# Attention scores as three fp32r passes on 64 rows, and projections pinned between the units of an attention

## The chip, the cores and the metric

One core of a Trainium2 chip. TensorE (PE, with its weight loads shown as PEld), VectorE (DVE), ScalarE (ACT) and GpSimd (POOL) each take their instructions in order and wait for each other through semaphores; SyncE (SP) issues the transfers. The metric is the time of one launch on the device in microseconds; lower is better.

## The reference

A chain of two blocks on 256 tokens of width 1024, all in fp32. The first block (convolution, retention, gated feed-forward, gate) is not touched. The second has two layers on the tokens ("lat") and, in the first layer, on 256 context tokens ("ctx"):

```python
# layer 0: differential attention, 8 heads, each with two score maps of 64 channels
q_l, k_l = apply_rope(q_l, cos, sin), apply_rope(k_l, cos, sin)   # lat only
s = einsum('bqhmd,bkhmd->bhmqk', q_blk, k) * 64 ** -0.5           # m = 0, 1
p = softmax(s);  p = p[:, :, 0] - lam * p[:, :, 1];  o = p @ v    # v: 128 channels
o = rmsnorm(o, subln) * (1 - lam_init);  y = o.reshape(...) @ wo
# lat queries read ctx and lat keys (512), ctx queries read ctx keys (256)
# layer 1: neighbourhood attention, 16 heads of 64 channels, lat queries only
s = concat([q @ k_lat * 64 ** -0.5 + bias (masked), q @ k_ctx * 64 ** -0.5])   # 512 keys
o = softmax(s) @ v;  y = o.reshape(...) @ wo
# after each: h = h + g * y, then a gated feed-forward on rmsnorm(h)
```

## The kernel before

Activations lie with channels on the 128 partitions and tokens in the columns. A projection is a sum of three fp32r products (`mm3`, or `mm3_tok` with tokens and weights exchanged): weights and activations are each split into a rounded part `hi` and the rest `lo`, and hi x hi, hi x lo and lo x hi are summed in PSUM. `weights` loads a tile of 1,024 or 768 columns into one of four buffers `raw`, and makes `hi` on ScalarE (L129) and `lo` on VectorE (L130), five buffers each. One such tile of 1,024 is 24 matmuls of 256 columns.

A scheduler puts each engine's instructions in order when the kernel is built. It goes by the order in the program and fills what is not ready yet with later work; `tc.issue_after(ins)` keeps instructions behind one of the same engine. The order is then fixed: on the chip an engine that waits holds all that is behind it.

**Layer 0.** `early_qk` and `early_v` project the context of head pairs c = 0 to 2 before the tokens are ready. For c = 0 to 3 the main loop then projects the tokens' q and k (128 channels are one head's two maps, j is the head of the pair), rotates them in fp32 (`rope`: L731 to L734, four VectorE steps), projects v, and calls `da_heads`. The projections of pair c + 1 follow the units of pair c in the program, so they are what TensorE has for its waits. `da_unit` works on one head and one block of 128 queries, 32 in all: two score products (L757), one for each map, each in plain fp32 from 64 of the partitions (q and k rows 0 to 63 or 64 to 127), each into one of two PSUM banks `s`; for each map a maximum (L761) and its scaling (L762) on VectorE and an exponential with its sum (L764) on ScalarE; a few one-column steps (L767 to L769); the combination of the two maps (L770); transposes on TensorE (L773), a copy (L775), the product with v (L780); and the RMS norm of the result (L783 to L787, with GpSimd's power at L785), which a later unit's `flush` transposes into `po_all`. The outputs of pairs 0 to 2 are kept as `raws` and split after the last projection, because the split tiles use the ring of the projections' inputs. `wo_first(0)` is the first part of the output projection, eight pieces of 18 matmuls, after all units. `ada_dve(0, 3, ...)` is 16 products on VectorE (L256) for a modulation vector of the next norm.

**Layer 1.** For each c (four heads), q is scaled and cut into `hi` and `lo` halves for each head, laid on opposite halves of the partitions, and k gets three tiles in the same way, by 12 ScalarE and 8 VectorE instructions on half tiles. `na_scores` then needs two matmuls a head and query block (32 in all): one over 128 rows (L989), which sums hi x hi and lo x hi, and one over 64 rows (L990) for hi x lo. Bias (L992), maximum, exponential and scaling follow, then transposes and the product with v. Each head's bias table is fetched into one of three buffers when its head comes.

## Time and profile before

| | |
|---|---|
| median of 3 runs | 1448.93 us (1446.19 to 1449.93) |
| the profiled execution | 1450.36 us, span 1448.1 us |
| busy in the span | PE 1410.9, PEld 1262.8, DVE 1075.4, ACT 700.5, POOL 34.1 us |
| mean granted TensorE clock | 0.991 |
| score products of layer 0 (L757) | 455.3 to 637.9 us, 128 matmuls |
| score products of layer 1 (L989, L990) | 1064.6 to 1229.8 us, 64 matmuls |

The span is from the first to the last instruction of the profiled execution. A matmul's busy time covers its way through the pipeline, so that matmuls overlap; the distance between starts is the rate. A plain fp32 matmul shows as two.

### The profile page before, as it was taken

The numbers are of one execution on the slowest core, as the hardware profiler recorded it, in microseconds if no ns is written. First come the engines' busy times: TensorE is split into PE (matmuls) and PEld (weight loads), VectorE is DVE, ScalarE is ACT, GpSimd is POOL, SyncE is SP. The second block draws the span as 40 slices with busy tenths as digits, with TensorE's granted clock in tenths as the row PEclk, the third lists the DMA queues.
The fourth block names the chain that finished last, engine by engine and source line by source line (L and its number), as shares of the span: only waits on it lengthen the run. The fifth ranks groups of instructions, "written<-read, shape, count | busy, mean of one in ns | idle before, by whom it ended". The sixth has DMA issues, their size and how long they took to land.

```text
span 1448.1 us, 25617 instructions
## 1 busy us (share of the span) xinstructions
PE 1410.9 (97%) x9811; PEld 1262.8 (87%) x9811; DVE 1075.4 (74%) x2333; ACT 700.5 (48%) x1323; POOL 34.1 (2%) x52
## 2 busy tenths in 40 slices
PE   7998999999999999999999999999999999999997
PEld 6898899999998887589888888889988778899997
DVE  7975889985778785778699999965775576676653
ACT  5655544454554545754432222323565555654442
POOL 0000000000000010110000000000000000000000
PEclk9999899999999999999999999999999999999998
DMA  8457498677554331034466676634632233355562
GB/s 289 128 168 255 169 318 275 218 215 221 167 175 146 131 96 32 7 103 160 132 215 198 210 239 218 210 123 129 203 99 87 74 88 119 132 182 182 153 180 91
DMA packets 76874, 236.66 MB, mean 163 GB/s; under 512 B 8656, under 2 KB 13008, under 8 KB 76624
## 3 DMA queue, kind: packets, MB, share of 16 engines
q1 hardware_dynamic: 76752, 235.03, 50.6%
q8 instruction: 77, 1.26, 0.3%
q14 instruction: 45, 0.37, 0.1%
HBM read 233.95 MB, written 1.05 MB: 162 GB/s over the span
## 4 chain that ended last, share of the span: by engine, by line
PE 80%; issue 13%; DMA 2%; DVE 2%; ACT 1%; SPq 0%; POOL 0%; DVEq 0%; POOLq 0%; ACTq 0%
PE mm L161 19%; PE mm L162 19%; PE mm L163 19%; PE s L757 3%; PE mm L172 2%; PE mm L171 2%; PE mm L170 2%; PE t L780 2%; PE o L1022 1%; DMA raw<-w_in 1%; PE s L162 1%; PE s L161 1%; PE s L163 1%; PE t L1012 1%; PE s L990 1%
## 5 line engine op out<-in xcount | busy, mean ns | idle before, releaser
L129 ACT CAST hi<-raw 128x1024 fp32r<-128x1024 f32 (+2 forms) x376 | 358.8, 956 | 547.8 <-PE mm L162 345.7
L130 DVE TENSOR_TENSOR lo<-raw,hi 128x1024 fp32r<-128x1024 f32 (+2 forms) x376 | 415.5, 1106 | 158.1 <-ACT hi L129 154.6
L161 PE MATMUL mm<-x,hi 128*128 128x256 f32 (+2 forms) x1568 | 486.3, 314 | 13.0 <-ACT x L151 7.9
L162 PE MATMUL mm<-x,hi 128*128 128x256 f32 (+2 forms) x1568 | 487.4, 312 | 1.3 <-DVE x L612 1.0
L163 PE MATMUL mm<-x,lo 128*128 128x256 f32 (+2 forms) x1568 | 487.5, 312 | 0.8 <-DVE lo L130 0.8
L161 PEld LDWEIGHTS mm<-x,hi 128*128 128x128 f32 x1568 | 299.9, 193 | 39.7 <-issue 11.4
L163 PEld LDWEIGHTS mm<-x,lo 128*128 128x128 f32 x1568 | 301.9, 193 | 23.5 <-issue 8.6
L162 PEld LDWEIGHTS mm<-x,hi 128*128 128x128 f32 x1568 | 301.9, 193 | 22.2 <-issue 6.1
L256 DVE SCALAR_TENSOR_TENSOR junk<-adaw,sb 128x512 f32<-128x512 f32 x320 | 220.2, 688 | 12.9 <-DMA adaw<-ada 8.5
L161 PE MATMUL mm<-o,hi 128*128 128x256 f32 (+1 forms) x356 | 105.3, 300 | 0.7 <-ACT o L147 0.5
L162 PE MATMUL mm<-o,hi 128*128 128x256 f32 (+1 forms) x356 | 105.6, 298 | 0.0
L163 PE MATMUL mm<-o,lo 128*128 128x256 f32 (+1 forms) x356 | 105.3, 297 | 0.0
L163 PE MATMUL s<-x,lo 128*128 128x258 f32 (+1 forms) x288 | 81.9, 284 | 0.0
L161 PE MATMUL s<-x,hi 128*128 128x258 f32 (+1 forms) x288 | 81.8, 284 | 0.0
L162 PE MATMUL s<-x,hi 128*128 128x258 f32 (+1 forms) x288 | 81.8, 284 | 0.0
L162 PE MATMUL mm<-q,hi 128*128 128x256 f32 (+1 forms) x265 | 81.0, 306 | 0.0
L163 PE MATMUL mm<-q,lo 128*128 128x256 f32 (+1 forms) x265 | 80.9, 305 | 0.0
L161 PE MATMUL mm<-q,hi 128*128 128x256 f32 (+1 forms) x265 | 80.9, 305 | 0.0
L161 PEld LDWEIGHTS mm<-o,hi 128*128 128x128 f32 x356 | 67.4, 191 | 5.4 <-issue 1.7
L162 PEld LDWEIGHTS mm<-o,hi 128*128 128x128 f32 x356 | 68.0, 191 | 2.6 <-issue 0.5
L163 PEld LDWEIGHTS mm<-o,lo 128*128 128x128 f32 x356 | 68.0, 191 | 1.9 <-issue 0.2
L172 PE MATMUL mm<-hi,x 128*128 128x256 f32 x240 | 69.1, 288 | 0.0
(250 smaller groups left out, 2153.9 us busy)
## 6 DMA issues: line engine op xcount, KB each, us to landing
raw<-gu SPq DMA_DIRECT2D x88, 512.0 KB, 3.9
adaw<-ada SPq DMA_DIRECT2D x80, 512.0 KB, 4.5
raw<-wqkv SPq DMA_DIRECT2D x66, 512.0 KB, 4.3
raw<-ffn SPq DMA_DIRECT2D x44, 512.0 KB, 5.6
raw<-down SPq DMA_DIRECT2D x37, 384.0 KB, 3.2
raw<-down SPq DMA_DIRECT2D x37, 320.0 KB, 3.0
raw<-w_in SPq DMA_DIRECT2D x22, 512.0 KB, 5.3
o<-ada SPq DMA_DIRECT2D x32, 256.0 KB, 5.9
```

Source lines behind the costliest of these rows:

```text
L129: last_conv[:] = [act.copy(hi[:, :n], raw[:, :n]).ins, dve.tensor_tensor(lo[:, :n], raw[:, :n], f32(hi[:, :n]), op=ALU.subtract).ins]
L130: dve.tensor_tensor(lo[:, :n], raw[:, :n], f32(hi[:, :n]), op=ALU.subtract).ins]
L161: pe.matmul(out, wh, xh, start=first and k == 0, stop=False)
L162: pe.matmul(out, wh, xl, start=False, stop=False)
L163: last_mm[0] = pe.matmul(out, wl, xh, start=False, stop=last and k == n - 1).ins
L170: pe.matmul(out, xh[:, ts_], wh, start=k == 0, stop=False)
L171: pe.matmul(out, xh[:, ts_], wl, start=False, stop=False)
L172: pe.matmul(out, xl[:, ts_], wh, start=False, stop=k == n - 1)
L256: dve.scalar_tensor_tensor(out=junk, in0=raw[:, gs_], scalar=1.0, in1=sb[:, v, gs_], op0=ALU.mult, op1=ALU.mult, accum_out=acc[:, n, v, g: ...
L757: pe.matmul(o, q[ms, qs], k[ms, k0:k0 + n], start=True, stop=True)
L780: mm = pe.matmul(po[:, :P], pT[:, j * P:(j + 1) * P], vv, start=j == 0, stop=j == nk - 1)
L990: pe.matmul(ps, q[rows, qs], k[2][rows], start=False, stop=True)
```

## The change

Both attentions now split q and k into `hi` and `lo` tiles and make each score map of three fp32r matmuls on 64 rows, hi x hi, hi x lo and lo x hi. The two maps (or two heads) that share a tile are alternated, so that consecutive matmuls use opposite halves of the rows and different banks. `both_free` orders the first matmul of a unit behind the `reciprocal` of the one before it, which follows both exponentials. The scale 1/8 moves into the split of q, and the maximum is negated by the reduction, so that L762 and L994 go; two one-column steps of the norm move to GpSimd.

In layer 0 the projections are cut into pieces of 24 matmuls (one weight tile) and handed to `da_heads` as `fill`: each is traced after one unit, and its matmuls are kept behind that unit's last score matmul. The context's projections of pair 3 become such pieces too, the q and k of a pair are made one head at a time, and `wo_first(0)` becomes eight pieces behind the units of pair 3. The splits of `raws` move: three after the first head of pair 1, one straight from PSUM, two after pair 2. In layer 1 both bias tables of a pair of heads are fetched ahead of its scores.

```diff
-EARLYN = 9
+WO_AT = {1: (0,), 2: (1, 2), 3: (3,), 4: (4,), 5: (5,), 6: (6,), 7: (7,)}
...
+    last_exp = [None]
+    def both_free(mm):
+        if last_exp[0] is not None:
+            tc.add_manual_dep(mm.ins, last_exp[0].name, mybir.DependencyInfo(
+                mybir.DependencyClass.NoSync, mybir.DependencyReason.DATA), reason="both banks")
...
-        p, ps = [], []
-        for m in range(2):
-            ms = slice(64 * m, 64 * m + 64)
-            o = bank(pss, "s")[:, :n]
-            pe.matmul(o, q[ms, qs], k[ms, k0:k0 + n], start=True, stop=True)
-            ps.append(o)
+        (qh, ql), (kh, kl) = q, k
+        ps = [bank(pss, "s")[:, :n] for _ in range(2)]
+        for i, (a_, b_) in enumerate(((qh, kh), (qh, kl), (ql, kh))):
+            for m in range(2):
+                ms = slice(64 * m, 64 * m + 64)
+                mm = pe.matmul(ps[m], a_[ms, qs], b_[ms, k0:k0 + n], start=i == 0, stop=i == 2)
+                if i + m == 0:
+                    both_free(mm)
+        last_s = mm.ins
+        p = []
         for m in range(2):
             o = ps[m]
-            dve.tensor_reduce(out=sc[:, m:m + 1], in_=o, axis=AX.X, op=ALU.max)
-            dve.tensor_scalar(out=sc[:, 2 + m:3 + m], in0=sc[:, m:m + 1], scalar1=-0.125, scalar2=None, op0=ALU.mult)
+            dve.tensor_reduce(out=sc[:, 2 + m:3 + m], in_=o, axis=AX.X, op=ALU.max, negate=True)
             e = tmp2("e", 3)
-            act.activation(e[:, :n], o, AF.Exp, bias=sc[:, 2 + m:3 + m], scale=0.125, accum_out=sc[:, 4 + m:5 + m])
+            act.activation(e[:, :n], o, AF.Exp, bias=sc[:, 2 + m:3 + m], accum_out=sc[:, 4 + m:5 + m])
             p.append(e)
-        dve.reciprocal(sc[:, 7:8], sc[:, 5:6])
+        pool.tensor_tensor(sc[:, 6:7], sc[:, 4:5], sc[:, 4:5], op=ALU.mult)
+        last_exp[0] = dve.reciprocal(sc[:, 7:8], sc[:, 5:6]).ins
         dve.scalar_tensor_tensor(out=sc[:, 8:9], in0=sc[:, 4:5], scalar=sc[:, 7:8], in1=nlam, op0=ALU.mult, op1=ALU.mult)
-        dve.scalar_tensor_tensor(out=sc[:, 6:7], in0=sc[:, 4:5], scalar=sc[:, 4:5], in1=epsc, op0=ALU.mult, op1=ALU.mult)
         dve.scalar_tensor_tensor(out=p[0][:, :n], in0=p[1][:, :n], scalar=sc[:, 8:9], in1=p[0][:, :n], op0=ALU.mult, op1=ALU.add)
...
-        dve.scalar_tensor_tensor(out=sc[:, 10:11], in0=sc[:, 9:10], scalar=1.0 / 128, in1=sc[:, 6:7], op0=ALU.mult, op1=ALU.add)
+        pool.tensor_scalar(out=sc[:, 10:11], in0=sc[:, 6:7], scalar1=128 * EPS, scalar2=sc[:, 9:10], op0=ALU.mult, op1=ALU.add)
...
+        return last_s
...
+    def qk_piece(c, grp, j):
+        def run(ins):
+            part_ = weights(a["wqkv0"][grp * 4 + c][:, j * 1024:(j + 1) * 1024], (1024,))
+            ps = bank(pmm, "mm")
+            with behind(ins):
+                mm3(ps[:, :T], per_k(part_, [KD], P), xl)
+            ring_ = "q" if (c, j) == (3, 1) else "o"
+            raw, hi, lo = tmp2(), slot(ring_, F32R), slot(ring_, F32R)
+            act.copy(raw[:, T:], early[c][grp][:, j * T:(j + 1) * T])
+            rope(raw, ps[:, :T])
+            if grp == 0:
+                split_scaled(raw, 0.125, hi, lo)
+            else:
+                split(raw, hi, lo)
+            QK[c][grp][j] = (hi, lo)
+        return run
...
+            ps, w = open_v[0]
+            with behind(ins):
+                mm3_tok(ps[:, jj * T:(jj + 1) * T], w, xl, CS[jj])
...
+        def fill_in(u, ins):
+            for f in fill.get(u, ()):
+                f(ins)
...
-            raw = slot("o")
-            act.activation(raw, po_all, AF.Copy, scale=sub8)
-            raws.append(raw)
-    for c in range(4):
...
-            if c < 2:
-                ps = bank(pmm, "mm")
-                for j in range(2):
-                    s = got[2 * grp + j]
-                    o = ps[:, j * T:(j + 1) * T]
-                    mm3(o, w[j], xl)
-                    rope(s, o)
-                    dst.append(s)
...
-        if c == 3:
-            for raw in raws:
-                hi, lo = slot("x", F32R), slot("x", F32R)
-                split(raw, hi, lo)
-                os_.append((hi, lo))
-        da_heads(c, q, k, v)
+    for f in (qk_piece(0, 0, 0), qk_piece(0, 1, 0), v_piece(0, 0), v_piece(0, 1)):
+        f(None)
+    for c in range(3):
+        fill = {0: [qk_piece(c, 0, 1)], 1: [qk_piece(c, 1, 1)], 4: [qk_piece(c + 1, 0, 0)], 5: [qk_piece(c + 1, 1, 0)]}
+        if c == 0:
+            fill.update({2: [early_piece(0, 0)], 3: [early_piece(0, 1)], 6: [v_piece(1, 0)], 7: [v_piece(1, 1)]})
+        elif c == 1:
+            fill[0].append(early_piece(1, 0))
+            fill[1].append(early_piece(1, 1))
+            fill.update({2: [early_piece(2, 0)], 3: [early_piece(2, 1)], 6: [v_piece(2, 0)], 7: [v_piece(2, 1)]})
+        else:
+            fill.update({2: [qk_piece(3, 0, 1)], 3: [qk_piece(3, 1, 1)], 6: [v_piece(3, 0)], 7: [v_piece(3, 1)]})
+        da_heads(c, fill)
         if c == ADA3 and 3 not in ADA_PE:
             ada_dve(0, 3, (last_load[0], last_mul[0]), range(ADA3N, KD), *acc3)
+    split_raws()
...
+    def wo_piece(v, n):
+        def run(ins):
+            if n % 2 == 0:
+                open_w[0] = weights(a["wo0a"][n // 2], (768, 768)), bank(pmm, "mm")
+            ws, ps = open_w[0]
+            o = ps[:, (n % 2) * T:(n % 2 + 1) * T]
+            with behind(ins):
+                mm3(o, per_k([ws[n % 2]], (6,), P), part(os_[:6], v))
+            resid(0, 2, n, o, v)
+        return run
     def wo_first(v):
         for n in range(KD):
-            if n % 2 == 0:
-                ws = weights(a["wo0a"][n // 2], (768, 768))
-                ps = bank(pmm, "mm")
-            o = ps[:, (n % 2) * T:(n % 2 + 1) * T]
-            mm3(o, per_k([ws[n % 2]], (6,), P), part(os_[:6], v))
-            resid(0, 2, n, o, v)
-    wo_first(0)
+            wo_piece(v, n)(None)
+    da_heads(3, {u: [wo_piece(0, n) for n in ns] for u, ns in WO_AT.items()})
...
-    def na_scores(q, k, jj, qt, bt):
-        rows = slice(64 * jj, 64 * jj + 64)
-        qs = slice(jj * T + qt * P, jj * T + (qt + 1) * P)
+    def na_scores(q, k, i, qt):
+        (qh, ql), (kh, kl) = q, k
+        qs = slice(i * T + qt * P, i * T + (qt + 1) * P)
+        ps = [bank(pss, "s") for _ in range(2)]
+        for n, (a_, b_) in enumerate(((qh, kh), (qh, kl), (ql, kh))):
+            for jj in range(2):
+                rows = slice(64 * jj, 64 * jj + 64)
+                mm = pe.matmul(ps[jj], a_[rows, qs], b_[rows], start=n == 0, stop=n == 2)
+                if n + jj == 0:
+                    both_free(mm)
+        return ps
+    def na_softmax(ps, qt, bt):
         sc = small.tile([P, 12], F32, tag="sc", name="sc", bufs=8)
-        ps = bank(pss, "s")
-        pe.matmul(ps, q[:, qs], k[jj], start=True, stop=False)
-        pe.matmul(ps, q[rows, qs], k[2][rows], start=False, stop=True)
         b0 = 128 if qt == 0 else 0
         dve.tensor_tensor(ps[:, :T], ps[:, :T], bt[:, b0:b0 + T], op=ALU.add)
-        dve.tensor_reduce(out=sc[:, 0:1], in_=ps, axis=AX.X, op=ALU.max)
-        dve.tensor_scalar(out=sc[:, 1:2], in0=sc[:, 0:1], scalar1=-1.0, scalar2=None, op0=ALU.mult)
+        dve.tensor_reduce(out=sc[:, 1:2], in_=ps, axis=AX.X, op=ALU.max, negate=True)
         e = tmp2("e", 3)
         act.activation(e, ps, AF.Exp, bias=sc[:, 1:2], accum_out=sc[:, 2:3])
-        dve.reciprocal(sc[:, 3:4], sc[:, 2:3])
+        last_exp[0] = dve.reciprocal(sc[:, 3:4], sc[:, 2:3]).ins
         dve.tensor_scalar(out=e, in0=e, scalar1=sc[:, 3:4], scalar2=None, op0=ALU.mult)
...
+            bts = []
             for jj in range(2):
-                bt = tmp2()
-                nc.sync.dma_start(out=bt[:, :384], in_=a["rpb"][4 * c + 2 * i + jj])
-                for qt in range(2):
-                    e = na_scores(q[i], k[i], jj, qt, bt)
+                bts.append(tmp2())
+                nc.sync.dma_start(out=bts[jj][:, :384], in_=a["rpb"][4 * c + 2 * i + jj])
+            for qt in range(2):
+                ps = na_scores(q, k[i], i, qt)
+                for jj in range(2):
+                    e = na_softmax(ps[jj], qt, bts[jj])
...
-            s = slot("q", F32R)
-            for jj in range(2):
-                d = s[:, jj * T:(jj + 1) * T]
-                act.activation(d[H[jj]], o[H[jj]], AF.Copy, scale=0.125)
-                dve.scalar_tensor_tensor(
-                    out=d[H[1 - jj]], in0=o[H[jj]], scalar=0.125, in1=f32(d[H[jj]]), op0=ALU.mult, op1=ALU.subtract)
-            q.append(s)
+            mm3(ps[:, j * T:(j + 1) * T], w[j], xl)
+        q, k = (slot("q", F32R), slot("q", F32R)), []
+        split_scaled(ps, 0.125, *q)
...
-            s = [slot("q", F32R) for _ in range(3)]
-            for jj in range(2):
-                for r in (jj, 1 - jj):
-                    act.copy(s[jj][H[r]], ps[H[jj]])
-                dve.tensor_tensor(s[2][H[jj]], ps[H[jj]], f32(s[jj][H[jj]]), op=ALU.subtract)
+            s = slot("q", F32R), slot("q", F32R)
+            split(ps, *s)
```

## Rows read from the trace of the kernel before

**Rows 1.** Page, chain that ended last: shares of the span by engine.
```profile
PE 80%; issue 13%; DMA 2%; DVE 2%; ACT 1%; SPq 0%; POOL 0%; DVEq 0%; POOLq 0%; ACTq 0%
```

**Rows 2.** Windows (us): length; PE, PEld, DVE, ACT, POOL busy (count); clock; DMA share; GB/s.
```profile
455.00:578.00 123.00, 123.00 (x815) 98.88 (x814) 92.19 (x278) 66.56 (x172) 9.91 (x16) 1.00 0.29 90
578.00:612.00 34.00, 30.85 (x158) 18.57 (x157) 23.49 (x83) 23.91 (x78) 4.32 (x8) 1.00 0.05 15
...
500.00:540.00 40.00, 40.00 (x274) 33.29 (x274) 32.76 (x106) 20.20 (x53) 3.65 (x5) 1.00 0.27 80
1140.00:1180.00 40.00, 40.00 (x253) 32.03 (x252) 22.48 (x48) 20.81 (x45) 0.00 (x0) 1.00 0.26 75
```

**Rows 3.** Timeline, TensorE, differential scores: start, length (us), line, operands, count.
```profile
455.33 1.13 PE L757 MATMUL s<-q 64*128 64x512 f32 x4
...
461.89 0.28 PE L161 MATMUL mm<-x,hi 128*128 128x256 f32 x1
462.01 0.28 PE L162 MATMUL mm<-x,hi 128*128 128x256 f32 x1
462.22 1.12 PE L757 MATMUL s<-q 64*128 64x512 f32 x2
463.27 0.39 PE L163 MATMUL mm<-x,lo 128*128 128x256 f32 x1
463.49 0.28 PE L161 MATMUL mm<-x,hi 128*128 128x256 f32 x1
...
471.74 0.28 PE L171 MATMUL mm<-lo,x 128*128 128x256 f32 x1
471.95 0.70 PE L757 MATMUL s<-q 64*128 64x256 f32 x2
...
472.80 0.28 PE L170 MATMUL mm<-hi,x 128*128 128x256 f32 x1
```

**Rows 4.** Timeline, loads of weights for the product at 462.22.
```profile
462.21 0.29 PEld L757 LDWEIGHTS s<-q 64*128 64x128 f32 x2
```

**Rows 5.** Timeline, TensorE, neighbourhood scores.
```profile
1072.20 0.39 PE L989 MATMUL s<-q 128*128 128x512 f32 x1
1072.52 0.50 PE L990 MATMUL s<-q 64*128 64x512 f32 x1
1072.95 0.39 PE L161 MATMUL mm<-x,hi 128*128 128x256 f32 x1
1073.18 0.28 PE L162 MATMUL mm<-x,hi 128*128 128x256 f32 x1
```

**Rows 6.** Groups by line and shape, 440 to 660: count | busy us, mean ns | idle before.
```profile
L130 DVE TENSOR_TENSOR lo<-raw,hi 128x1024 fp32r<-128x1024 f32 x21 | 25.6, 1220 | 2.0 <-ACT hi L129 1.9
L761 DVE TENSOR_REDUCE sc<-s 128x1 f32<-128x512 f32 x32 | 22.1, 689 | 9.1 <-PE s L757 8.2 <-POOL sc L785 0.8
...
L761 DVE TENSOR_REDUCE sc<-s 128x1 f32<-128x256 f32 x32 | 13.4, 422 | 9.5 <-PE s L757 9.0
L770 DVE SCALAR_TENSOR_TENSOR e<-e,sc 128x512 f32<-128x512 f32 x16 | 12.0, 750 | 0.3
L256 DVE SCALAR_TENSOR_TENSOR junk<-adaw,sb 128x512 f32<-128x512 f32 x16 | 11.0, 685 | 0.0
L762 DVE TENSOR_SCALAR sc<-sc 128x1 f32<-128x1 f32 x64 | 9.4, 148 | 0.3
L770 DVE SCALAR_TENSOR_TENSOR e<-e,sc 128x256 f32<-128x256 f32 x16 | 7.7, 481 | 0.2
...
L769 DVE SCALAR_TENSOR_TENSOR sc<-sc,epsc 128x1 f32<-128x1 f32 x32 | 6.9, 215 | 4.7 <-ACT e L764 4.5
L734 DVE TENSOR_TENSOR q<-rp 128x256 f32<-128x256 f32 x16 | 6.7, 417 | 0.7 <-PE t L780 0.7
...
L148 DVE TENSOR_TENSOR x<-o,x 128x512 fp32r<-128x512 f32 x6 | 4.1, 688 | 1.2 <-ACT x L147 1.0
...
L785 POOL TENSOR_TENSOR sc<-sc,mhalf 128x1 f32<-128x1 f32 x32 | 18.6, 580 | 202.2 <-DVE sc L784 116.5 <-DVE sc L762 85.7
```

More of the change, by code (lines that the diff above doesn't have):

```diff
@@ L639, in body @@
     down("down1", fs, ep)
-    early = [], [], []
+    early = [], [], [], []
     def early_qk(c, grp):
@@ L661, in early_v @@
             mm3_tok(ps[:, j * T:(j + 1) * T], w, xc, CS[j])
-        s = slot("q" if c < 2 else "o")
+        s = slot("q")
         act.copy(s, ps)
         early[c].append(s)
-    steps = [lambda c=c, i=i: early_v(c) if i == 2 else early_qk(c, i) for c in range(3) for i in range(3)][:EARLYN]
+    steps = [lambda c=c, i=i: early_v(c) if i == 2 else early_qk(c, i) for c in range(3) for i in range(3)]
     def early_some(i, j):
@@ L789, in da_unit, with behind @@
         late.append((po_all[:, at:at + P], on))
-    os_, raws = [], []
-    def da_heads(c, q, k, v):
+        return last_s
+    QK = [[[None] * 2 for _ in range(2)] for _ in range(4)]
+    V = [[] for _ in range(4)]
+    def behind(ins):
+        return tc.issue_after(ins) if ins is not None else nullcontext()
+    def qk_piece(c, grp, j):
[14 more added lines that the diff above has]
+        return run
@@ new lines, in body, with v_piece, early_piece, run @@
+    open_v = [None]
+    def v_piece(c, jj):
+        def run(ins):
+            if jj == 0:
+                open_v[0] = bank(pmm, "mm"), w_wide(a["wqkv0"][8 + c])
+            ps, w = open_v[0]
+            with behind(ins):
+                mm3_tok(ps[:, jj * T:(jj + 1) * T], w, xl, CS[jj])
+            if jj == 1:
+                s = slot("q")
+                act.copy(s, ps)
+                V[c] += [s, early[c][2]]
+        return run
+    open_e = [None]
+    def early_piece(i, j):
+        def run(ins):
+            if j == 0:
+                src = a["wqkv0"][i * 4 + 3]
+                open_e[0] = bank(pmm, "mm"), w_wide(src) if i == 2 else w_blocks(src)
+            ps, w = open_e[0]
+            o = ps[:, j * T:(j + 1) * T]
+            with behind(ins):
+                if i == 2:
+                    mm3_tok(o, w, xc, CS[j])
+                else:
+                    mm3(o, w[j], xc)
+            if j == 1:
+                s = slot("q")
+                act.copy(s, ps)
+                early[3].append(s)
+        return run
@@ L794, in da_heads, with split_raws @@
+    os_, raws = [], []
+    def split_raws():
+        for raw in raws:
+            hi, lo = slot("x", F32R), slot("x", F32R)
+            split(raw, hi, lo)
+            os_.append((hi, lo))
+        raws.clear()
+    def da_heads(c, fill):
+        def fill_in(u, ins):
+            for f in fill.get(u, ()):
+                f(ins)
         if c == 3:
-            parts = [(slot("o", F32R), slot("o", F32R)) for _ in range(2)]
+            parts = [(slot("x", F32R), slot("x", F32R)) for _ in range(2)]
+            u = 0
@@ new lines, in da_heads @@
+            if c == 1 and i == 0:
+                raw = slot("q")
+                act.activation(raw, po_all, AF.Copy, scale=sub8)
+                raws.append(raw)
+                split_raws()
+            elif c == 1:
+                hi, lo = slot("x", F32R), slot("x", F32R)
+                split_scaled(po_all, sub8, hi, lo)
+                os_.append((hi, lo))
+            else:
+                raw = slot("q")
+                act.activation(raw, po_all, AF.Copy, scale=sub8)
+                raws.append(raw)
@@ L1025, in na_heads @@
             os_.append((s[:, :T], s[:, T:]))
-    H = slice(0, 64), slice(64, 128)
     for c in range(4):
```

68 lines of the change are left out of this document (17 added, 51 removed).

## The prediction

> **What bounds the kernel now.** I read the chain that ended last first, then the busy times of two stretches, then the TensorE timeline step by step. The chain is TensorE for 80% of the span [rows 1]. Busy time alone says too little, because matmuls overlap in the pipeline; the reader should look at the distance from one matmul's start to the next. In a dense run of 256-column fp32r matmuls that step is 0.12 us, and every score product breaks the rhythm [rows 3]. In differential attention TensorE is dense from 455 to 578 us, with VectorE busy 92.2 of 123 us (75%; the densest slice, 500 to 540 us, has 82%). From 578 to 612 us, where the projections have run out, TensorE has 158 matmuls and 3.2 us with none running [rows 2]. So a score product that gets cheaper shortens the end directly, as long as VectorE and ScalarE deliver the softmax in time.
>
> **Scores of differential attention.** There are 32 units (8 heads, 4 blocks of queries): 16 "lat" units with 512 keys, 16 "ctx" units with 256. Each has two 64-row products in plain fp32, each of which runs as two passes. A 512-key product alone: without it the matmuls at 463.27 and 463.49 would have followed 462.01 by 0.12 and 0.24, as that one follows 461.89; it costs 463.49 - 462.01 - 0.24 = 1.24 us. A 256-key one, with one matmul left out of the rows before 472.80, costs 472.80 - 471.74 - 0.24 = 0.82 [rows 3]. The 0.42 between them is 256 columns in two passes, so an fp32 pass takes 0.21 for 256 columns, and 0.82 - 0.42 = 0.40 is fixed, paid at the change between 128-row and 64-row matmuls. Where both halves of a unit stand side by side, four passes take 1.13 us where two take 1.12 [rows 3]: the two row halves run at the same time. On the timeline 6 such pairs and 52 single products stand (27 of 512 keys, 25 of 256 alone). A pair costs what its longer half costs: 4 hold a 512-key product, 2 do not. Before: 31 x 1.24 + 27 x 0.82 = 60.6 us.
>
> After, a unit is six fp32r passes, alternating between the halves, so three passes' time and one change of mode. An fp32r pass of 256 columns is 0.12. For 512 columns the neighbourhood scores tell it: a 128-row and a 64-row product together cost 1073.18 - 1072.20 - 0.12 = 0.86 [rows 5] (the first, at 1072.20, would itself have been the next step), which is two passes and the fixed 0.40, so 0.23 a pass. A lat unit: 0.40 + 3 x 0.23 = 1.09; a ctx unit: 0.40 + 3 x 0.12 = 0.76. After: 16 x 1.85 = 29.6 us. **Saved: 31.0 us.** Bounds: nothing hides better than this from below; from above, if the fp32r halves did not overlap, six passes make 1.78 and 1.12, 46.4 us, 14.2 saved.
>
> The three passes need their weights loaded behind a running pass in the same half. The row for the fp32 product shows it: its two loads lie within 0.29 us, while its first pass runs until 462.75 (0.53 after its start, by half of the 1.05 to the next matmul) [rows 3, 4]. The Trainium skill's TensorE: Matmul & The Clock Gate, Part 3 (The mechanism), says in its list of what overlaps that a load runs beside a matmul only when the row groups differ. By that rule passes two and three would each show a load, at most the 0.12 that a load and its matmul take in a dense run: 32 x 0.24 + 16 x 0.24 = 11.5 us less saved. The trace disagrees for fp32; for fp32r no row shows it. I take the trace.
>
> **Scores of neighbourhood attention.** 32 products of 0.86 are 27.5 us [rows 5]; 16 pairs of 1.09 are 17.4. **Saved: 10.1 us.** The half-tile copies that made its operands go too (per block of heads 12 ScalarE and 8 VectorE instructions become 3 and 3). That stage has VectorE at 22.5 of 40 us [rows 2], so this is worth nothing by itself. Against it: both bias tables of a pair are now fetched together from three buffers, so the second waits for the previous pair's last use, and loads of weights queue behind it on SyncE. Between nothing (four loaded tiles lie ahead) and one tile's 24 matmuls, 2.9 us, I take 1.5.
>
> **What VectorE gains and pays.** Gone: 64 scalings (0.15 each, 9.4 us) and 64 small products (32 of 0.22, 6.9 us, and 32 more of one column) [rows 6]. New: 16 splits of a rotated q or k tile, at the 0.69 of L148: 11 us, and as many ScalarE copies, which has room (66.6 of 123 busy, rows 2). Two one-column operations move to GpSimd: one is off the path, the other adds between nothing and the 0.58 of the power there [rows 6] ahead of ScalarE's normalisation, in place of 0.15 to 0.22 on VectorE. It is behind the value product, a whole unit from its use, so I cost it at nothing; if ScalarE, which takes its work in order, stood still for it, 32 x 0.4 = 13 us of ScalarE's idle time would go.
>
> **The order.** Pieces of 24 matmuls (2.88 us) are pinned behind a unit's scores, 18-matmul pieces (2.16) of the output projection behind the last head's units. This fills the hole at 578 to 612: 3.2 us [rows 2]. But a unit's first score now waits until the previous unit has finished both exponentials, since it needs both banks. So units run in rounds. TensorE's work in 32 rounds: 26 pieces of 2.88, 8 of 2.16, the scores' 29.6, and transposes and value products, 13 steps a lat unit and 7 a ctx unit at no more than 0.12: 74.9 + 17.3 + 29.6 + 38.4 = 160.2 us, **5.0 a round**. VectorE's in the same rounds [rows 6]: 16 lat units of 2 x 0.69 + 0.75 + 0.22 + 0.15 = 2.50; 16 ctx of 2 x 0.42 + 0.48 + 0.37 = 1.69; 14 q or k pieces of 1.22 (weights) + 4 x 0.42 (rotation) + 0.69 (split) = 3.59; 12 other weight tiles of 1.22; 8 output pieces of 0.92 (768 columns, from the 1,024) + 0.48; ten further splits, 6.0; the modulation vector's 16 products, 11.0. Sum 67.0 + 50.3 + 14.6 + 11.2 + 6.0 + 11.0 = 160.1, **also 5.0**. VectorE is thus level with TensorE, where before it had a quarter free. The rounds with q or k pieces are worst: 2.50 + 3.59 = 6.1 of VectorE against 1.09 + 1.56 + 2.88 = 5.5 of TensorE.
>
> From below a round is 5.0. From above: a lat round cannot be shorter than 1.09 + 2 x 0.69 + an exponential (nearest row: L770's 512 columns, 0.75) + 0.2 of hand-overs = 3.4, and if all other VectorE work of the round came after it in turn, a q or k round is 7.0 and the others about 4.6, mean 5.65, with the modulation vector and splits 6.1. That is VectorE 82% busy, just the densest slice of before. I take 5.4 (93% of VectorE), nearer the lower end, since rotations and weights have no reader in the same round and the modulation vector can slide later. (The last head's first unit has no piece behind it; a hole of at most 3.4 - 1.1 us there is within this.)
>
> **The sum.** Same work before: 160.2 + 31.0 + 3.2 = 194.4; after 32 x 5.4 = 172.8; saved 21.6. Neighbourhood attention: 10.1 - 1.5 = 8.6. The profiled execution took 1450.36 (span 1448.1 and 2.3 around it): 1450.4 - 30.2 = 1420.2. The median of the runs is 1.4 below that execution, so **1419 us**.
>
> **Rivals.**
> 1. Rounds are as short as TensorE allows (5.0): 34.2 + 10.1 saved, 1405. For: nothing queued on VectorE is late by more than one operation. Against: it needs VectorE at 100%.
> 2. VectorE takes over as the bound, rounds of 5.65 to 6.1: 13.6 to -0.8 saved there, 1427 to 1441. For: the sum above. Against: in the densest slice TensorE still did not wait. The Trainium skill names this in TensorEngine Tiling (Array Packing), PSUM Bottleneck: tiling speeds up the products but not the reading of PSUM, which may then be the limit.
> 3. The fp32r halves do not overlap (the change doesn't do what it says): 14.2 saved in differential attention and 27.5 - 16 x 1.78 = -1 in the other; with rounds then 5.5 on TensorE alone, 194.4 - 177 = 17, total about 16: 1433. Against: four passes in the time of two [rows 3].
> 4. Slower: holding both banks until the second exponential makes rounds longer than (194.4 + 8.6) / 32 = 6.34 us. From there on the kernel loses; at 7.0, the worst round worked out above, in every unit, it is 21 us slower: 1470. Against: it needs more than the fully serial 6.1, so ScalarE's waits for GpSimd or weight loads on top.
>
> **Chances.** Forecast, rounds of 5.2 to 5.6 (1412 to 1425): 0.52. Rival 1: 0.15. Rival 2: 0.22. Rival 3: 0.05. Rival 4: 0.06. Leaving out rival 4, the upper part of rival 2 and the lowest edge, the range is 1403 to 1437. A measurement of this kernel tells about 0.3%, 4.3 us, from no change. Faster takes rivals 1 and 3, the forecast and nearly all of 2: 0.90; same 0.04; slower 0.06.
>
> **What would show it.** Score matmuls whose starts come in pairs a few ns apart, three pairs within about 0.9 us (lat) and 0.5 (ctx); 32 groups of six where 58 stood; no hole at the last head's units. The round: first to last score over 31 rounds, 167 us by the forecast. If VectorE is 90% or more busy there and TensorE's waits end on the exponentials or on L770's successor, the 5.4 is right in kind. The prediction is wrong if the scores come singly, if the six stand longer than 1.3 us, or if TensorE's waits in differential attention sum to more than 35 us.

## The result, and the profile after

The changed kernel takes 1423.63 us (median of 4 runs, 1420.28 to 1424.95) against 1448.40 for the kernel before on the same chip (4 runs, 1446.19 to 1449.93): ratio 0.9827, 95% interval 0.9804 to 0.9849, or 24.8 us less. The forecast was 1419, its range 1403 to 1437. The profiled execution took 1420.28 us. On its page, the span and the chain by engine (TensorE's share stays, [rows 1]):

```profile
span 1418.4 us, 25707 instructions
...
PE 79%; issue 14%; ACT 2%; DVE 2%; DMA 2%; POOL 1%; SPq 0%; POOLq 0%; DVEq 0%; ACTq 0%
```

**Where the time went.** Windows that follow one another tell it. Their borders are the same events in both kernels: the first load of layer 0's down-projection, the first differential score, and the sums of three norms (behind differential attention, and at the two ends of neighbourhood attention). The columns are those of [rows 2]; first the kernel before:

```profile
0.00:269.80 269.80, 251.72 (x2071) 233.94 (x2072) 217.79 (x442) 147.32 (x267) 6.55 (x11) 0.97 0.68 230
269.80:455.30 185.50, 183.46 (x1524) 182.57 (x1523) 136.97 (x256) 96.76 (x156) 3.92 (x3) 1.00 0.60 190
455.30:648.90 193.60, 190.45 (x1228) 148.73 (x1228) 146.06 (x446) 114.10 (x316) 18.55 (x32) 1.00 0.25 77
...
1045.70:1254.20 208.50, 205.08 (x1363) 169.69 (x1362) 133.72 (x290) 117.80 (x258) 0.70 (x1) 1.00 0.31 95
```

The changed kernel:

```profile
0.00:264.60 264.60, 248.68 (x2071) 231.06 (x2072) 217.62 (x441) 147.61 (x267) 6.77 (x11) 0.98 0.69 235
264.60:451.90 187.30, 179.17 (x1460) 178.29 (x1458) 134.92 (x251) 98.04 (x157) 2.09 (x3) 0.97 0.58 183
451.90:629.50 177.60, 172.50 (x1361) 156.24 (x1361) 148.88 (x347) 127.56 (x344) 50.06 (x96) 0.98 0.34 108
...
1026.10:1224.90 198.80, 197.11 (x1395) 167.37 (x1394) 118.28 (x238) 100.66 (x223) 0.70 (x1) 1.00 0.32 100
...
451.90:614.30 162.40, 157.78 (x1236) 141.85 (x1236) 136.71 (x319) 117.83 (x313) 45.06 (x87) 0.98 0.36 113
...
1049.80:1200.10 150.30, 150.30 (x1023) 123.47 (x1022) 88.28 (x177) 76.57 (x174) 0.00 (x0) 1.00 0.32 98
```

The differences of these stages are -5.2, +1.8, -16.0 and -9.7. The stage between (396.8 and 396.6) and the last (193.9 and 193.5) give -0.2 and -0.4; with 0.4 outside the span this makes the 30.1 between the two profiled executions. The 5.2 fall where the code is the same (in the profiles of the experiments below this stage, never changed, took 265.3 to 269.8), and they are about the difference between the 30.1 and the medians' 24.8. The second stage is the surprise: it has 64 matmuls fewer (7.7 us at 0.12), and is longer. The last two rows are the stretches from first to last score: TensorE never stands still in neighbourhood attention, and VectorE is busy 136.7 of 162.4 us (84%) in differential attention.

**The scores**, which answer to [rows 3, 4] and [rows 5]; matmuls and loads, a unit of 512 keys, one of 256, and a pair in neighbourhood attention:

```profile
457.93 0.28 PE L170 MATMUL mm<-x,lo 128*128 128x256 f32 x1
...
458.13 0.53 PEld L757 LDWEIGHTS s<-o 64*128 64x128 f32 x6
458.14 0.96 PE L757 MATMUL s<-o 64*128 64x512 f32 x6
...
459.03 0.39 PE L168 MATMUL mm<-x,hi 128*128 128x256 f32 x1
459.25 0.28 PE L169 MATMUL mm<-x,hi 128*128 128x256 f32 x1
...
483.22 0.28 PE L170 MATMUL mm<-x,lo 128*128 128x256 f32 x1
483.43 0.62 PE L757 MATMUL s<-o 64*128 64x256 f32 x6
...
484.21 0.28 PE L178 MATMUL mm<-lo,x 128*128 128x256 f32 x1
...
1059.59 0.96 PE L1055 MATMUL s<-q 64*128 64x512 f32 x6
1060.48 0.50 PE L170 MATMUL mm<-x,lo 128*128 128x512 f32 x1
```

Costed as the prediction costed [rows 3], six 512-key passes take 459.25 - 457.93 - 0.24 = 1.08 us and six 256-key passes 484.21 - 483.22 - 0.24 = 0.75. The sum had 1.09 and 0.76. All six loads lie within 0.53 us, behind running passes of the same row halves. The Trainium skill's TensorE: Matmul & The Clock Gate, Part 3 (The mechanism), has in its list of what overlaps that a load overlaps only across row groups. For fp32r too the trace disagrees with that item, and the 11.5 us that hung on it were not lost.

Not every group stands like this. Of the 32 groups of differential attention 25 take at most 0.91 us from the first of the six to the next matmul, five take 1.5 to 2.2. In three of these the second half waits for an exponential of the unit before, 2.1 us in all, although the first half has started. This is the rest of a group whose first matmul started at 467.82:

```profile
468.91 0.62 PE L757 MATMUL s<-o 64*128 64x256 f32 x5 [0.70 <-ACT e L766]
```

So `both_free` fixes TensorE's order when the kernel is built, and is no wait on the chip. In neighbourhood attention 13 of the 16 pairs take at most 0.91 us; in the other three (2.34 us each) eight transposes stand between the halves.

### The profile page after: what moved, and what is told of

It reads as the page before. It is cut to its first block, busy times and chain, and to the rows that moved or that the text cites. A ratio compares the mean times of both kernels' runs of the same rounds, so it can differ in the third digit from the quotient of the medians.

```text
span 1418.4 us, 25707 instructions
## 1 busy us (share of the span) xinstructions
PE 1376.9 (97%) x9907; PEld 1260.0 (89%) x9907; DVE 1060.8 (75%) x2174; ACT 697.1 (49%) x1314; POOL 64.8 (5%) x116
## 4 chain that ended last, share of the span: by engine, by line
PE 79%; issue 14%; ACT 2%; DVE 2%; DMA 2%; POOL 1%; SPq 0%; POOLq 0%; DVEq 0%; ACTq 0%
PE mm L168 20%; PE mm L169 19%; PE mm L170 19%; PE mm L177 2%; PE mm L178 2%; PE mm L179 2%; PE s L757 1%; PE o L1095 1%; PE t L782 1%; PE s L169 1%; PE s L170 1%; PE s L168 1%; PE s L1055 1%; PE t L1085 1%; ACT hi L129 1%
## 5 line engine op out<-in xcount | busy, mean ns | idle before, releaser
L129 ACT CAST hi<-raw 128x1024 fp32r<-128x1024 f32 (+2 forms) x382 | 365.2, 958 | 520.0 <-PE mm L169 327.3
L130 DVE TENSOR_TENSOR lo<-raw,hi 128x1024 fp32r<-128x1024 f32 (+2 forms) x382 | 422.3, 1107 | 173.3 <-ACT hi L129 170.2
L168 PE MATMUL mm<-x,hi 128*128 128x256 f32 (+2 forms) x1584 | 491.8, 314 | 13.3 <-ACT x L151 8.0
L168 PEld LDWEIGHTS mm<-x,hi 128*128 128x128 f32 x1584 | 303.0, 193 | 42.3 <-issue 14.5
L168 PE MATMUL mm<-o,hi 128*128 128x256 f32 (+1 forms) x340 | 100.9, 303 | 2.3 <-ACT o L147 2.1
L169 PE MATMUL mm<-o,hi 128*128 128x256 f32 (+1 forms) x340 | 101.5, 300 | 0.0
L168 PE MATMUL s<-x,hi 128*128 128x258 f32 (+1 forms) x304 | 86.2, 284 | 0.0
L169 PE MATMUL s<-x,hi 128*128 128x258 f32 (+1 forms) x304 | 86.2, 284 | 0.0
L170 PE MATMUL s<-x,lo 128*128 128x258 f32 (+1 forms) x304 | 86.2, 283 | 0.0
L168 PEld LDWEIGHTS mm<-o,hi 128*128 128x128 f32 x340 | 65.2, 195 | 5.9 <-ACT o L147 2.8
L177 PE MATMUL mm<-hi,x 128*128 128x256 f32 x240 | 70.1, 292 | 0.0
L194 POOL TENSOR_TENSOR rv<-rv,mhalf 128x2 f32<-128x2 f32 (+1 forms) x16 | 14.5, 907 | 1200.3 <-DVE rv L193 1200.3
L179 PE MATMUL mm<-hi,x 128*128 128x256 f32 x240 | 69.1, 288 | 0.0
```

The lines of the kernel that those rows point to most:

```text
L129: last_conv[:] = [act.copy(hi[:, :n], raw[:, :n]).ins, dve.tensor_tensor(lo[:, :n], raw[:, :n], f32(hi[:, :n]), op=ALU.subtract).ins]
L130: dve.tensor_tensor(lo[:, :n], raw[:, :n], f32(hi[:, :n]), op=ALU.subtract).ins]
L168: pe.matmul(out, wh, xh, start=first and k == 0, stop=False)
L169: pe.matmul(out, wh, xl, start=False, stop=False)
L170: last_mm[0] = pe.matmul(out, wl, xh, start=False, stop=last and k == n - 1).ins
L177: pe.matmul(out, xh[:, ts_], wh, start=k == 0, stop=False)
```

## The experiments

The brackets give the range of the runs, then the ratio to the kernel before on the same chip (medians 1447.4 to 1448.4) and its 95% interval. The changed kernel's 1423.63 was measured apart from these, so differences of medians to it of less than about 4 us are not told apart. Stretches of the profiles repeat better: from first to last neighbourhood score it is 150.3 us in the changed kernel and in the nine below that leave that attention as it is.

**Half after half.** Per half its three passes in a row, instead of alternating.

```
-        for i, (a_, b_) in enumerate(((qh, kh), (qh, kl), (ql, kh))):
-            for m in range(2):
+        for m in range(2):
+            for i, (a_, b_) in enumerate(((qh, kh), (qh, kl), (ql, kh))):
```

> The changed kernel with the six passes of a unit's scores in another order, in both attentions: the three of one row half, then the three of the other. Theory (matmuls start in program order, so only neighbours in the order overlap): the second half starts beside the first half's third pass, five passes' time: 1.09 becomes 1.55 and 0.75 becomes 1.0, 32 units and 16 pairs make 18.6 us: 1438 to 1444 us, with starts at about 0, 0.34, 0.57 and then the second half. Rival (each row half goes on by itself, as the plain fp32 pairs of the kernel before showed two passes of each half side by side): starts still in pairs, no change, 1420 to 1427 us.

1425.53 us (1423.51 to 1429.25; 0.9854, 0.9825 to 0.9884). The timeline of one 512-key unit:

```profile
458.82 0.97 PE L757 MATMUL s<-o 64*128 64x512 f32 x6
459.72 0.39 PE L168 MATMUL mm<-x,hi 128*128 128x256 f32 x1
```

From the first of the six to the next matmul it is 0.90, against 0.89 in the alternating order: the second half's products do not wait for the first half's three. The halves run at the same time in either order; the alternation isn't what buys it.

**Plain fp32 products, pinned pieces kept.** One fp32 product per half, its operands not split.

```
-                mm = pe.matmul(ps[m], a_[ms, qs], b_[ms, k0:k0 + n], start=i == 0, stop=i == 2)
+            mm = pe.matmul(ps[m], q[ms, qs], k[ms, k0:k0 + n], start=True, stop=True)
...
-            QK[c][grp][j] = (hi, lo)
+            QK[c][grp][j] = raw
```

> The changed kernel with the differential scores in plain fp32 again, the two maps side by side; q and k are not split, the maximum is scaled by its own instruction again. Theory (the saving in differential attention comes from the two row halves running at once, not from fp32r): a unit's scores cost 1.24 and 0.82 us in place of 1.09 and 0.75, 3.4 us more of TensorE in 32 units; VectorE loses 16 splits (11 us) and gets 64 scalings (9 us): 1424 to 1429 us. Rival (the fp32r passes are the saving): the products come singly at 1.24 and 0.82 each, 31 us more: 1450 to 1456 us.

1438.15 us (1437.09 to 1439.37; 0.9934, 0.9913 to 0.9955), between the two. A unit whose halves run together, one whose second half is late, and the stretch from first to last score:

```profile
460.15 1.13 PE L755 MATMUL s<-o 64*128 64x512 f32 x4
461.21 0.39 PE L168 MATMUL mm<-x,hi 128*128 128x256 f32 x1
...
465.60 1.24 PE L755 MATMUL s<-o 64*128 64x256 f32 x4
466.78 0.39 PE L168 MATMUL mm<-x,hi 128*128 128x256 f32 x1
...
456.00:632.90 176.90, 169.58 (x1191) 141.24 (x1191) 138.62 (x371) 112.33 (x303) 42.59 (x91) 0.99 0.34 106
```

Together, four passes take 1.06 where six fp32r passes take 0.89, for 16 such units 2.7 us. But the stretch is 14.5 us longer, as is the median. The second unit shows part of it (1.18 for 256 keys): its second half's weights are loaded only after an exponential of the unit before.

```profile
466.15 0.29 PEld L755 LDWEIGHTS s<-o 64*128 64x128 f32 x2 [0.25 <-ACT e L765]
```

In this kernel loads for scores wait 17 times for an exponential, 6.7 us in all, in the changed one three times, 3.0 us. Neither theory nor rival holds as a whole, and the rest of the 14.5 isn't settled.

**Neighbourhood attention as before**, the rest changed (scores, operands and bias fetches of layer 1 from the kernel before).

> The changed kernel with the whole of neighbourhood attention as before. Theory (its 32 products of 0.86 us became 16 pairs of 1.09 on the path that sets the end): 8 to 11 us slower than the changed kernel, 1432 to 1435 us, and first to last neighbourhood score 10 us or more longer than 150. Rival (that stage's time went to its softmax rounds or its transfers, and the cheaper scores were hidden): within 4 us of the changed kernel.

1432.39 us (1431.54 to 1433.74; 0.9895, 0.9874 to 0.9916): 8.8 more. Its stretch from first to last score is 164.80 long, against 150.30; the whole stage between the sums of the two norms, which also holds the projections left over, takes 208.6 against 198.8.

**No rule for both banks.**

```
-        if last_exp[0] is not None:
+        if False:
```

> The changed kernel without the rule that a unit's first score waits for both exponentials of the unit before. Theory: the rule costs and gains little, since the rounds are set by the work in them; with it gone the first half's three passes can start one exponential earlier (up to 0.75 us) while the second half waits, so some groups open by 0.2 to 0.7 us between the first starts of the halves and the rounds stay at about 5.2: 1420 to 1428 us. Rival: what the rule keeps together is what makes a group cheap; without it the second half of most units starts when the first has finished, a lat group lasts 1.78 instead of 1.09 and a ctx group 1.12 instead of 0.76, and the kernel takes 16 x 1.05 = 17 us more: 1437 to 1443.

1436.19 us (1431.41 to 1436.48; 0.9912, 0.9894 to 0.9931): 12.6 more, and the theory falls. Two units in the timeline, one in each attention, and the two stretches:

```profile
583.26 0.96 PE L757 MATMUL s<-o 64*128 64x512 f32 x3
584.16 0.44 PE L775 MATMUL t<-tab,e 128*128 128x128 f32 x2
584.53 0.96 PE L757 MATMUL s<-o 64*128 64x512 f32 x3
...
1063.91 0.96 PE L1055 MATMUL s<-q 64*128 64x512 f32 x3
...
1067.29 0.96 PE L1055 MATMUL s<-q 64*128 64x512 f32 x3
...
456.50:622.30 165.80, 162.93 (x1242) 146.14 (x1242) 138.53 (x321) 119.80 (x316) 49.91 (x89) 0.97 0.36 109
1057.10:1216.90 159.80, 159.80 (x1011) 125.66 (x1010) 88.58 (x178) 75.92 (x175) 0.00 (x0) 1.00 0.30 91
```

TensorE's order, laid down when the kernel is built, now puts other work between the halves, in 12 of the 16 pairs of neighbourhood attention (three with the rule) and in 6 of the 32 units of differential attention (none with it). Three passes of one half alone take the same 0.9 as six of both. Neighbourhood attention loses 9.5 us of its gain, differential attention 3.4. The rule that the prediction feared for the rounds is what keeps the pairs together, above all in neighbourhood attention.

**No pins.** The pieces keep their place in the program and may run as soon as they can.

```
-        return tc.issue_after(ins) if ins is not None else nullcontext()
+        return nullcontext()
```

> The changed kernel without the pins: the pieces are traced after the same units, but their matmuls are no longer kept behind a unit's scores. Theory (the pins keep projections back for the softmax waits): the pieces run as early as their inputs allow, the gap of 2.7 us ahead of the first scores closes, but the units of the third head pair run dry; 2 to 6 us slower than the changed kernel, 1426 to 1430 us. Rival (the pins only cost, because they starve the start): the start gap closes and nothing is lost later; 3 to 8 us faster, 1416 to 1421 us.

1435.05 us (1432.63 to 1440.59; 0.9918, 0.9889 to 0.9947): 11.4 more. First to last score takes 174.8 us against 162.4, the stage in front of it 190.3 (265.3 to 455.6) against 187.3, and the hole of [rows 2] is back, larger:

```profile
562.00:606.00 44.00, 34.75 (x196) 25.63 (x195) 32.10 (x87) 27.72 (x90) 13.10 (x31) 0.84 0.14 45
```

**More work for VectorE.** One product that nobody reads, between the reciprocal and the combination.

```
+        extra = tmp2("junk", 1)
+        dve.tensor_tensor(extra[:, :n], p[0][:, :n], p[1][:, :n], op=ALU.mult)
```

> The changed kernel with one more VectorE product of two SBUF tiles per unit of differential attention (512 columns in 16 units, 256 in 16; about 0.6 and 0.35 us, 15 us in all), whose result nobody reads; it stands in VectorE's queue between the reciprocal and the combination of the two halves. Theory that VectorE is not the bound: only the two 20-us windows from 555 to 595 us have VectorE above 90% busy, so there 2 x 2.0 us do not fit, and the rest adds to the chain of a unit but not to TensorE's work: 2 to 6 us more, 1425 to 1430. Rival that VectorE sets the length of the rounds: all 15 us show, 1436 to 1440.

1447.08 us (1443.87 to 1449.06; 0.9992, 0.9983 to 1.0001): 23.5 more, beyond both. Two windows each, split at the nineteenth unit's first score; first the changed kernel, then this one:

```profile
451.90:547.90 96.00, 94.60 (x753) 86.20 (x753) 76.40 (x167) 70.71 (x183) 25.42 (x49) 0.98 0.38 124
547.90:614.30 66.40, 63.18 (x486) 55.65 (x485) 60.31 (x153) 47.11 (x131) 19.65 (x39) 0.97 0.32 98
```

```profile
456.00:554.20 98.20, 96.09 (x753) 86.66 (x753) 82.33 (x181) 70.00 (x183) 27.41 (x50) 0.98 0.39 121
554.20:641.60 87.40, 72.05 (x488) 61.65 (x487) 68.57 (x168) 48.94 (x132) 21.48 (x38) 0.84 0.24 73
```

Up to there VectorE works 5.9 us more and the stretch grows by 2.2: the amount of its work isn't the bound. Behind it the stretch grows by 21 us, more than the added work. VectorE's timeline there shows why:

```profile
604.64 0.68 DVE L263 SCALAR_TENSOR_TENSOR junk<-adaw,sb 128x512 f32<-128x512 f32 x1
...
611.60 0.75 DVE L774 SCALAR_TENSOR_TENSOR e<-e,sc 128x512 f32<-128x512 f32 x1
```

From the first of these rows seven of the modulation vector's products stand in the queue ahead of one unit's combination, and TensorE waits 7.0 us for it. The edit itself brings this about: the added product writes to `junk`, of which there is one buffer, and the modulation vector's products write to the same one (L260). All of them are ahead of the last pair's first added product (610.9 us), while in the changed kernel four combinations stand between them (575.0, 581.1, 586.3 and 593.1 us). So behind the eighteenth unit this run shows what a bad place in VectorE's queue costs, and not what 15 us of work cost.

**Those products elsewhere** (behind the first pair's rotations: ADA3 = 0 instead of 2).

> The changed kernel with the modulation vector's last 16 VectorE products (11 us) put behind the last rotation of the first pair of heads instead of the third, so that they fall near 475 to 515 us, where VectorE has 3.7 to 4.5 us free in each 20, and not at 555 to 600 us, where it is 93 to 96% busy. Theory that VectorE limits the rounds only where it is full: the 3.2 us in which TensorE stands still between 555 and 595 us and the low clock after them go (3 to 6 us less), and little is lost at the new place: 1418 to 1421 us. Rival: TensorE's holes there come from the chain of the last head's first units, which have less behind them, or the products cost the same wherever they stand: 1422 to 1426.

1421.75 us (1418.88 to 1423.74; 0.9816, 0.9801 to 0.983). TensorE is busy 38.51 us of 555 to 595 instead of 36.78, and 38.05 of 495 to 535, where they now stand, instead of 40.00. First to last score is 161.4 against 162.4. By the medians no gain can be told: nearer to the rival.

**Scale-and-add back on VectorE.**

```
-        pool.tensor_scalar(out=sc[:, 10:11], in0=sc[:, 6:7], scalar1=128 * EPS, scalar2=sc[:, 9:10], op0=ALU.mult, op1=ALU.add)
+        dve.tensor_scalar(out=sc[:, 10:11], in0=sc[:, 6:7], scalar1=128 * EPS, scalar2=sc[:, 9:10], op0=ALU.mult, op1=ALU.add)
```

> The changed kernel with the second of the two operations moved to GpSimd, the scale-and-add ahead of the power, back on VectorE. Theory (the prediction's): its place is worth nothing, since the normalisation that waits for it has a whole unit until its result is used; ScalarE's waits for GpSimd (13.3 us in all after the change, 8.6 before) shrink, VectorE does about 32 x 0.2 = 6.7 us more: 1422 to 1427. Rival that ScalarE, standing still for GpSimd, delays the next unit's exponentials and with them the round: 4 to 8 us less, 1416 to 1420.

1426.82 us (1425.88 to 1427.86; 0.9851, 0.9835 to 0.9867), at the upper end of the theory's range. The median alone, 3.2 more, doesn't tell the two kernels apart, but first to last score takes 166.5 instead of 162.4, although ScalarE's waits for GpSimd fall from 13.3 to 3.8 us. VectorE now stands still for ScalarE's sums of squares (L785), which come just ahead of the operation, 3.5 us in all.

**Before the first unit: three kernels.** TensorE's waits between 360 and 452 us in the changed kernel (us in all, times, the longest; the three largest):

```profile
PE s L757 <- ACT o L147: 2.4, 1, 2.4
PE mm L168 <- ACT o L147: 1.7, 1, 1.7
PE mm L168 <- ACT x L618: 1.6, 1, 1.6
```

First, early steps kept back for the norms:

```
+    hold[0] = st0.mm
+    early_some(2, 3)
...
+    early_some(3, 7)
+    hold[0] = st.mm
+    early_some(7, 9)
```

> The changed kernel with TensorE work kept back for the two norms that it idles in before the first unit: the 48 matmuls of the third early step of the context's q, k and v are pinned behind the sums of the norm at 366 us, and the last two early steps (96 matmuls) behind the sums of the norm at 428 us. Theory that the gaps (1.4 + 1.9 us at 366 to 370, 1.9 + 1.6 us at 432 to 437) are there because the early steps, no longer held up by their buffers, ran ahead of the norms and left nothing behind them: both gaps close, and the low clock that follows them goes too (two stretches of 6.8 and 3.4 us at half clock, some 1 to 4 us): 5 to 9 us less, 1415 to 1419. Rival: the norm's own chain on ScalarE and VectorE was late by itself, and matmuls moved behind the sums only leave the wait elsewhere (in front of the sums, or at the first piece): 0 to 2 us less, 1422 to 1425.

1422.19 us (1416.82 to 1422.72; 0.9824, 0.9808 to 0.9841). The first gap closes; the second moves in front of the sums, where TensorE waits 3.7 us. Second, six pieces ahead of the first unit:

```
-    for f in (qk_piece(0, 0, 0), qk_piece(0, 1, 0), v_piece(0, 0), v_piece(0, 1)):
+    for f in (qk_piece(0, 0, 0), qk_piece(0, 1, 0), v_piece(0, 0), v_piece(0, 1), qk_piece(0, 0, 1), qk_piece(0, 1, 1)):
```

> The changed kernel with six pieces in front of the first unit instead of four: the two q and k pieces of the first two units run unpinned, and those units have none behind them. Theory: TensorE's 2.7 us without work just before the first score, where it waits for the first rotated and split q and k, get filled, and the second unit is short of 24 matmuls only for a round that the softmax of two neighbours shortens anyway: 2 to 4 us less, 1419 to 1422. Rival: a stretch without pieces costs as much at the first two units (a round of 512 keys cannot be shorter than about 3.4 us, against 1.1 + 1.6 of TensorE work without a piece, so 0.7 each, and the lead of VectorE is lost) as it saves before: no change, 1423 to 1426.

1424.74 us (1424.22 to 1429.5; 0.9848, 0.983 to 0.9867): the rival. The stage in front of the first score grows to 191.0 (269.8 to 460.8), so its gap isn't filled. The second unit's scores come 3.8 us after the first's, with no piece between, and wait 2.84 us for the exponentials:

```profile
460.80 0.96 PE L757 MATMUL s<-o 64*128 64x512 f32 x6
464.61 2.58 PE L757 MATMUL s<-o 64*128 64x512 f32 x6 [2.84 <-ACT e L766]
```

Third, one step kept back at each norm, and ADA3 = 0:

> The changed kernel with three corrections together: the third early step pinned behind the sums of the norm at 366 us, only the last early step (48 matmuls) pinned behind the sums of the norm at 428 us, and the modulation vector's late products behind the first pair of heads. Theory: the first two close the gaps before the first unit without opening one in front of the second norm's sums (kept back by two steps, TensorE waited 3.95 us there), worth 4 to 7 us, and the third adds its 3 to 5: 1412 to 1418, faster than both kernels. Rival: the norms' chain decides when the first unit can start, whatever TensorE does meanwhile, and the products cost the same anywhere: 1420 to 1425.

1417.32 us (1416.88 to 1421.18; 0.9793, 0.9778 to 0.9807). The best of all, 31 us below the kernel before; against the changed kernel 6 us by the medians, but the intervals of the two ratios still touch. Last, on top of it, the two early pieces of the last pair's queries, which need no current token, in front of the first unit:

> The kernel with the three corrections, and the two pieces of the last pair's context queries taken from behind the third and fourth unit and put, unpinned, in front of the first one (48 matmuls, 5.8 us), where that kernel's trace shows TensorE without work for 5.7 us while the first rotated q and k are split. They need nothing of the current tokens, so they can fill that wait. Theory that the rounds behind which they stood are set by TensorE (256 keys: 2.9 us of piece, 0.8 of scores, 0.8 of transposes and value products against a softmax of about 3.4): both rounds get shorter by about 1 us, and the clock does not fall in the wait: 2 to 5 us less, 1412 to 1415. Rival, as with six pieces first: the wait's end is set by ScalarE and VectorE, which now also have two weight tiles more to split ahead of it, and the first rounds are as long with no piece behind them: no change, 1416 to 1420.

1420.24 us (1419.29 to 1424.97; 0.9812, 0.9796 to 0.9828): the rival. The stage in front of the first score, and first to last score, in the kernel with three corrections and in this one:

```profile
266.10:450.30 184.20, 176.27 (x1459) 174.72 (x1457) 134.88 (x252) 98.35 (x157) 2.97 (x3) 1.00 0.59 186
450.30:610.60 160.30, 156.84 (x1238) 141.60 (x1238) 137.36 (x319) 118.38 (x317) 47.02 (x89) 0.98 0.35 111
```

```profile
268.50:453.00 184.50, 182.01 (x1506) 180.55 (x1505) 135.91 (x252) 99.17 (x158) 2.98 (x3) 1.00 0.60 186
453.00:616.90 163.90, 155.60 (x1195) 138.10 (x1194) 136.81 (x320) 118.31 (x316) 46.80 (x89) 0.96 0.35 109
```

47 matmuls more fit into the same 184.5 us. The first unit's start is set by the chain of norms, first projections, rotations and splits; TensorE's work there is slack. And the stretch behind, with 43 matmuls fewer, is 3.6 us longer. Its first four rounds, from which the two pieces are gone, take 21.8 us, against 21.7: they aren't set by TensorE's work either. The five behind them grow from 27.2 to 31.1; why, isn't shown.

## Why the prediction held, and what was mis-sized

**Scores of differential attention, 31.0 saved:** right for a group that stands together (1.08 and 0.75 measured for 1.09 and 0.76), as 25 of the 32 do. That a unit's first score waits for both exponentials was wrong: the chip starts the first half and holds the second, and five groups stand longer than the 1.3 us that the prediction took for a sign of being wrong. Rival 3, no overlap, is ruled out.

**Scores of neighbourhood attention, 8.6:** right. Undone, it costs 8.8. The stage gained 9.7, as the 10.1 of the scores alone: the 1.5 for the bias fetches was too much, and TensorE is busy for all of 150.3 us.

**VectorE's 5.0 a round:** a step that was wrong in method. The 160.1 added durations, but neighbouring VectorE operations overlap. From its timeline:

```profile
540.44 1.22 DVE L130 TENSOR_TENSOR lo<-raw,hi 128x1024 fp32r<-128x1024 f32 x1
541.59 0.16 DVE L770 RECIPROCAL sc<-sc 128x1 f32<-128x1 f32 x1
```

The 1.22 us split is followed after 1.15. From first to last score the groups' durations add up to 154.7 us, the busy time is 136.7, or 4.4 for each of 31 rounds. The Trainium skill's Perfetto Trace Analysis, DVE / Act Engine Instruction, says that a record ends at the acknowledgement of the writes, later than the point from which the next operation may start; these rows agree. Busy time by windows would have shown it before, as starts did for TensorE.

**The round, 5.4:** 162.4 / 31 = 5.24, so 32 rounds took 5 us less than forecast, and not for its reason. It had VectorE level with TensorE; VectorE has 4.4, and is busy 84% of the time where the prediction asked for 90% as a sign that the 5.4 is right in kind. In 25 of the 31 rounds TensorE never stands still, 17 of them in a row:

```profile
473.80:562.60 88.80, 88.80 (x726) 81.59 (x725) 74.63 (x166) 70.18 (x185) 27.12 (x52) 1.00 0.37 118
```

There TensorE's own work sets the round, as rival 1 had it, and the lengths 4.7, 5.0, 5.1 and 4.8 come back again and again. Beyond 31 rounds of 5.0 there are 7 us: TensorE's waits, 4.6 us in the other six rounds (35 was the sign of being wrong), and the granted clock of 0.98, by my estimate from that figure some 3 us. With little behind it a 512-key round takes 3.8 (six pieces first; forecast: no shorter than 3.4). Rival 2, a bound by VectorE's amount, is ruled out for the first eighteen units; rival 4, slower, didn't come.

**The operations on GpSimd, at nothing:** too low a gain. Back on VectorE, the scale-and-add costs 4.1 us from first to last score (3.2 by the medians).

**Pieces against the hole, 3.2:** right in kind; without pins 11.4 are lost, with a hole of 9.2 us between 562 and 606 and the clock at 0.84 there.

**Not in the sum: the start.** "Same work before: 194.4" took every moved matmul for 0.12 us saved where it had stood. The 64 matmuls gone from in front of the first unit, 7.7 us, shortened that stage by nothing; it grew by 1.8, 9.5 short. TensorE stands still for 8.1 us there instead of 2.0, and the granted clock is 0.97 instead of 1.00. Three kernels put the floor of this stage near 184.4 us: 184.3 with early steps kept back (266.6 to 450.9), 184.2 and 184.5 in the last two, with 1459 and 1506 matmuls in it. Before it was 185.5, with TensorE dense: its work and a chain like that one were about level, so that less of the one alone could bring 1 us or so. That is argued, for the chain before was another: it had no split of the first q and k. In the kernel with plain fp32 scores, which has none either, the stage takes 186.2 (269.8 to 456.0) instead of 187.3, so the splits are about 1 us of it. The corrections at the norms give back some 3 us of the stage.

**The balance.** Differential attention and its start gave 16.0 - 1.8 = 14.2 of the 21.6 forecast: 5 better by the rounds, 9.5 worse by the start, and 3 us less remain. They lie behind the last score, where the changed kernel has more matmuls left; from the last score's end to the sums of the norm, before and after:

```profile
638.20:648.90 10.70, 10.70 (x92) 10.70 (x92) 9.09 (x27) 6.34 (x22) 1.62 (x3) 1.00 0.07 27
614.90:629.50 14.60, 14.12 (x121) 13.93 (x119) 11.56 (x28) 9.13 (x29) 4.89 (x9) 1.00 0.20 55
```

Neighbourhood attention gave 9.7 for 8.6. Rounds of 5.24 put into the prediction's own sum make 1414. That the median, 1423.63, came within 5 us of the forecast is luck: the rounds were shorter than forecast, and the start and the end took that back and more. That the profiled execution came out at 1420.28, as summed, is chance as well: 5.2 of its gain lie in the unchanged first stage.

## What to carry to other kernels

Before work that is moved away from a place counts as saved there, look for the chain of dependent steps beside it: where the engine is dense and that chain as long, less work saves nothing. Add up engines by busy time in windows or by distances between starts, never by durations. When two half-array products share a time slot only if they are issued together, tie them together in the order: that rule alone was worth 12.6 us here.

## What the runs showed of the hardware

Products on the two row halves run side by side even if the program has all three passes of one half first: six take 0.90 us in either order, and three of one half alone also 0.9. Loads of weights for the second and third pass of a half lie hidden behind its running pass: six loads within 0.53 us. The power of one column on GpSimd took 0.68 us in the mean, with two more operations per unit there, against 0.58 [rows 6]. In the start, the granted clock was 0.83 from 360 to 380 us, with waits of TensorE of 1.2 and 1.7 us there, and 0.91 from 430 to 455, with waits of 1.6, 1.3 and 2.4, which is 1.2 GHz for a part of each and 2.4 for the rest.
